# Norms over features: squares of four feature tiles kept together, their four products with ones issued beside each other

## The chip, the cores and the metric

The kernel runs as one program on 1 core of one Trainium2 chip. The metric is device microseconds of one execution; all traces are of one profiled execution. The engines are named as in the profile: PE is TensorE's matmul, PEld its weight load, DVE VectorE, ACT ScalarE, POOL GpSimd, SP SyncE, which issues most DMAs.

## The reference, cut to what matters

Two blocks of two layers each work on 256 context tokens and 256 latent tokens with 1024 features. Before and after every mixer and feed-forward network stands a root-mean-square norm over the features of a token:

```python
def _rms(x, gain, eps=1e-6):
    xf = x.astype(jnp.float32)
    y = xf * lax.rsqrt(jnp.mean(xf * xf, axis=-1, keepdims=True) + eps)
    return (y * gain.astype(jnp.float32)).astype(x.dtype)
```

Between the norms stand linear layers (a gated linear recurrence with attention, feed-forward networks, a second recurrence, latent attention with retention, a state-space mixer). All arithmetic is kept near fp32: each weight and each activation is split into a high and a low part, and a product is three matmuls.

## The kernel before, in words

Activations lie feature-major: a tile `x` is 128 partitions by 8 feature tiles (`KT`) by tokens. `SEGS` names the two halves of the tokens, context (256) and latent (256). The mean square over the features is therefore a sum over partitions and over 8 feature tiles. Class `Squares` makes it. `add` (L63) is called once for each feature tile: ACT squares 128x256 elements into a tile `sq` (L70), and `flush` (L72) multiplies the square of the feature tile before it with 32 columns of ones on PE (L77). Feature tile `k` writes the 32 PSUM partitions from `32 * (k % 4)` on, so that the eight products fill four strips, each twice. `flush` is called at the start of the next `add`, and once more by `all_rows` (L86), which copies the sums to SBUF (DVE, L94), turns them into one number per token on PE (L97), takes the reciprocal root in 11 short DVE instructions (`rstd_rows`, L407 to L420), and `rstd` (L105) broadcasts it over the partitions on PE (L111). The tiles `sq` share two buffers of pool `sm`.

A norm stands in one of two surroundings. In the first, `add` is called from the consumer of a linear layer: `linear_steps` (L213) loads a tile of weights (L257, 512 KB), ACT rounds it to `hi` (L195), DVE makes `lo` (L196), PE runs 24 matmuls (L205 to L207) or twice as many halves, and the consumer copies or adds the PSUM tile into `y` or `x` and squares it. Seven linear layers do that: both output projections of the first block, both last feed-forward parts of the first block, the output projection and the feed-forward network of layer one of the second block, and the gated layer of the last mixer. Where both halves of the tokens are done, the last three tiles run all context halves first and then all latent halves, and the context's norm starts between them. In the second surrounding, `residual_scaled` (L501 to L509), outside a linear layer's consumer, DVE scales a tile of `y`, POOL or DVE adds it to `x` (L508), and `add` squares the result. `halves` (L511) runs this for the context and then for the latent half, twice in the first block.

The order of the instructions on each engine is fixed when the program is built, by a list scheduler with a model of durations: where an engine would idle, it takes later work whose inputs and buffers are there. So the loads and matmuls of the second block's modulation vectors (`mods_steps`, L319: loads `mraw` of 512 KB at L326, four strips of matmuls at L329), which stand in the program text only in the mixer of the second layer, are put far ahead of it. That stream has 16 loads of `ada_w`, and its tiles share the two buffers named `mraw` of pool `mp`. During the feed-forward network of the second block's first layer, `mods_rows` (L370) holds both of these buffers, and later loads of modulation weights use pools of their own.

Of the kernel before, what the change touches and what calls it, by code (L numbers as in the profile page):

```python
# [9 lines left out]
F32 = mybir.dt.float32  # L10
F32R = mybir.dt.float32r
I32 = mybir.dt.int32
AF = mybir.ActivationFunctionType
# [4 lines left out]
P = 128  # L18
D = 1024
KT = 8  # L20
# [36 lines left out]
class Squares:  # L57


    def __init__(self, K, N, kt, rows, tag):  # L60
        self.K, self.N, self.kt, self.rows, self.tag, self.k, self.ps, self.sq = K, N, kt, rows, tag, 0, None, None

    def add(self, src):  # L63
        K, N, rows, k = self.K, self.N, self.rows, self.k
        if k == 0:
            self.ps = K.psum(self.tag)
        self.flush()
        self.k += 1
        self.sq = K.sm.tile([P, 512], F32, tag="sq", name=K.n("sq"), bufs=2)
        K.nc.scalar.activation(self.sq[:rows, :N], src, AF.Square)  # L70

    def flush(self):  # L72

        K, N, rows, k = self.K, self.N, self.rows, self.k - 1
        if self.sq is not None:
            j = k % 4
            K.nc.tensor.matmul(self.ps[32 * j:32 * j + 32, :N], K.ones[:rows, :32], self.sq[:rows, :N], start=k < 4,  # L77
                               stop=k + 4 >= self.kt, skip_group_check=True)
        self.sq = None

    def token_rows(self):

# [46 lines left out]
class Kern:  # L129
# [1555 lines left out]
    def ffn(self, X, N, Wu, Wd, kind, y, pool, hbufs=12, after=None, between=None,  # L1685
# [6 lines left out]
        for b, wd in enumerate(Wd):  # L1692
# [36 lines left out]

            last = b == len(Wd) - 1  # L1730
            self.linear_fm(wd, (hi, lo), N, add, tick=ticks[1], ends=last, half=half if last else None)


# [120 lines left out]
def second(K, tc, xd, s2, part, sc, m0, X, out):  # L1854
# [5 lines left out]
    with tc.tile_pool(name="s5w", bufs=1) as wpool:  # L1860
        with tc.tile_pool(name="ffn2", bufs=1) as fp:
# [11 lines left out]
            acc = K.squares(SEGS)  # L1873
            bc = []
            K.linear_fm(A["bw_out"], M, T, add, ends=True, half=lambda: bc.append(acc[0].rstd()))
            K.dbg("x2a", x)
            X = K.norm_tiles(T)
# [256 lines left out]
```

## Time and profile before

| what | value |
|---|---|
| median of 3 runs | 2568.2 us (2568.14 to 2576.02) |
| profiled execution | 2566.27 us |
| span of its trace | 2563.7 us |
| PE busy | 2414.7 us (94%), 15813 matmul instructions |
| DVE busy | 1518.1 us (59%) |
| ACT busy | 971.3 us (38%) |
| POOL busy | 503.0 us (20%) |
| moved by DMA | 378.04 MB, mean 147 GB/s |

The time of an execution is the span plus what lies around it (2.6 us in the profiled one). Every fp32 product appears as two weight loads and two matmul instructions, so that the 160 products of L77 with 256 tokens are 320 instructions. An engine's busy share is an average over stages with different limits; a matmul's end is modelled, and the start of the next one tells what it cost.

### The profile page before, as it was taken

How to read it: one execution, taken by the hardware profiler on the slowest of the kernel's cores; microseconds unless marked ns; L12 is line 12 of the kernel's file. 1: busy time of each engine (PE TensorE's matmuls, PEld its weight loads, DVE VectorE, ACT ScalarE, POOL GpSimd, SP SyncE). 2: the span in 40 equal slices, each digit the busy share in tenths (PEclk: the TensorE clock that was granted, in tenths of full speed). 3: DMA queues.
4: the chain of work that ended last, by engine and by line, in shares of the span. 5: the costliest groups of instructions: out<-in, count | busy, mean ns of one | idle time of the engine just before them, and what ended most of it. 6: DMA issues, size and time to landing. Idle time of an engine off the chain costs nothing.

```text
span 2563.7 us, 40161 instructions
## 1 busy us (share of the span) xinstructions
PE 2414.7 (94%) x15813; PEld 1970.4 (77%) x15813; DVE 1518.1 (59%) x2897; ACT 971.3 (38%) x1591; POOL 503.0 (20%) x648
## 2 busy tenths in 40 slices
PE   6999989999999998889999999999999999948999
PEld 5885566888888688887799696546888888627999
DVE  5545436777853656673655533654688734585666
ACT  5523323322222433333444444443423224534543
POOL 2810012556630233230100100110100000360000
PEclk8999999999999999999999999989999999989999
DMA  8326673555552332123855431003365533976554
GB/s 279 122 95 230 226 279 108 160 163 167 161 145 91 106 124 67 59 82 136 282 178 182 154 110 60 9 17 105 111 188 181 165 99 104 200 254 212 156 181 149
DMA packets 162924, 378.04 MB, mean 147 GB/s; under 512 B 24144, under 2 KB 70096, under 8 KB 162608
## 3 DMA queue, kind: packets, MB, share of 16 engines
q1 hardware_dynamic: 159728, 368.27, 45.0%
q0 software_dynamic: 3008, 7.21, 1.0%
q8 instruction: 124, 2.03, 0.3%
q14 instruction: 64, 0.52, 0.1%
HBM read 344.75 MB, written 30.67 MB: 146 GB/s over the span
## 4 chain that ended last, share of the span: by engine, by line
PE 79%; DVE 10%; DMA 4%; ACT 3%; issue 2%; POOL 1%; SPq 0%; DVEq 0%; ACTq 0%; POOLq 0%
PE pl L205 18%; PE pl L206 18%; PE pl L207 17%; PE pm L329 3%; PE pl L984 2%; PE pa L77 2%; DVE lo L196 2%; DMA mcol<-ada_t 2%; PE pl L279 1%; PE pl L280 1%; DVE pm L395 1%; PE pl L277 1%; PE pb L77 1%; PE pa L661 1%; PE pl L1006 1%
## 5 line engine op out<-in xcount | busy, mean ns | idle before, releaser
L195 ACT CAST hi<-raw 128x1024 fp32r<-128x1024 f32 (+4 forms) x393 | 400.4, 1020 | 847.1 <-PE pl L206 555.0
L196 DVE TENSOR_TENSOR lo<-raw,hi 128x1024 fp32r<-128x1024 f32 (+4 forms) x393 | 496.6, 1265 | 332.2 <-ACT hi L195 330.2
L206 PE MATMUL pl<-X,hi 128*128 128x256 f32 (+1 forms) x2032 | 649.2, 321 | 6.2 <-POOL X L490 5.7
L205 PE MATMUL pl<-X,hi 128*128 128x256 f32 (+1 forms) x2032 | 651.3, 322 | 1.8 <-ACT X L487 1.8
L207 PE MATMUL pl<-X,lo 128*128 128x256 f32 (+1 forms) x2032 | 647.6, 320 | 0.8 <-DVE lo L196 0.7
L206 PEld LDWEIGHTS pl<-X,hi 128*128 128x128 f32 x2032 | 392.6, 194 | 37.4 <-POOL X L490 8.7
L205 PEld LDWEIGHTS pl<-X,hi 128*128 128x128 f32 x2032 | 391.9, 194 | 36.3 <-issue 6.9
L207 PEld LDWEIGHTS pl<-X,lo 128*128 128x128 f32 x2032 | 392.5, 193 | 31.5 <-issue 4.9
L206 PE MATMUL pl<-hl,hi 128*128 128x256 f32 (+1 forms) x1071 | 326.8, 306 | 6.7 <-DVE hl L1713 6.6
L205 PE MATMUL pl<-hh,hi 128*128 128x256 f32 (+1 forms) x1071 | 329.5, 309 | 3.4 <-ACT hh L1712 3.2
L207 PE MATMUL pl<-hh,lo 128*128 128x256 f32 (+1 forms) x1071 | 325.9, 305 | 0.0
L205 PEld LDWEIGHTS pl<-hh,hi 128*128 128x128 f32 x1071 | 202.4, 189 | 25.6 <-issue 7.1
L206 PEld LDWEIGHTS pl<-hl,hi 128*128 128x128 f32 x1071 | 202.6, 189 | 18.9 <-DVE hl L1713 8.7
L207 PEld LDWEIGHTS pl<-hh,lo 128*128 128x128 f32 x1071 | 202.7, 189 | 10.5 <-issue 0.4
L205 PE MATMUL pl<-M,hi 128*128 128x256 f32 (+1 forms) x416 | 125.4, 303 | 7.4 <-ACT hi L195 6.4
L1505 POOL TENSOR_TENSOR Ec<-PGr,bc 128x576 f32<-128x576 f32 x64 | 95.5, 1503 | 169.8 <-DMA bc<-s_w 89.0
L329 PE MATMUL pm<-mraw,s_cc 128*32 128x512 f32 x576 | 115.7, 606 | 11.3 <-DMA mraw<-ada_w 10.9
L207 PE MATMUL pl<-M,lo 128*128 128x256 f32 (+1 forms) x416 | 122.2, 295 | 1.2 <-DVE lo L196 1.2
L206 PE MATMUL pl<-M,hi 128*128 128x256 f32 (+1 forms) x416 | 122.8, 296 | 0.2 <-DVE M L856 0.2
L1726 DVE TENSOR_TENSOR y<-y,pl 128x256 f32<-128x256 f32 (+1 forms) x86 | 45.1, 525 | 115.9 <-PE pl L207 115.5
L490 POOL TENSOR_TENSOR X<-nt,X 128x256 fp32r<-128x256 f32 x48 | 37.5, 781 | 382.7 <-ACT nt L489 382.7
L395 DVE SCALAR_TENSOR_TENSOR pm<-mcol,mrow 128x512 f32<-128x512 f32 x128 | 89.2, 697 | 34.0 <-DMA mcol<-ada_t 21.7
(515 smaller groups left out, 3753.5 us busy)
## 6 DMA issues: line engine op xcount, KB each, us to landing
mraw<-mod_w SPq DMA_DIRECT2D x96, 512.0 KB, 5.5
raw<-f_u SPq DMA_DIRECT2D x88, 512.0 KB, 4.3
mraw<-ada_w SPq DMA_DIRECT2D x64, 512.0 KB, 6.3
raw<-p_u SPq DMA_DIRECT2D x64, 512.0 KB, 3.7
raw<-p_d SPq DMA_DIRECT2D x64, 512.0 KB, 3.6
raw<-ow_fm SPq DMA_DIRECT2D x32, 512.0 KB, 3.3
mcol<-ada_t SPq DMA_DIRECT2D x64, 256.0 KB, 3.0
raw<-f_d SPq DMA_DIRECT2D x32, 448.0 KB, 3.3
```

Source lines behind the costliest of these rows:

```text
L77: K.nc.tensor.matmul(self.ps[32 * j:32 * j + 32, :N], K.ones[:rows, :32], self.sq[:rows, :N], start=k < 4, stop=k + 4 >= self.kt, skip_gro ...
L195: nc.scalar.copy(hi, raw)
L196: nc.vector.tensor_tensor(lo, raw, f32(hi), ALU.subtract)
L205: mm(out, w[0][:, kw, wsl], xh, start=first and a == 0, stop=False, skip_group_check=True)
L206: mm(out, w[0][:, kw, wsl], xl, start=False, stop=False, skip_group_check=True)
L207: mm(out, w[1][:, kw, wsl], xh, start=False, stop=last and a == nk - 1, skip_group_check=True)
L329: nc.tensor.matmul(ps[32 * j:32 * j + 32, :], s[:, k, :], raw[:, jj * 512:(jj + 1) * 512], start=k == 0, stop=k == KT - 1, skip_group_chec ...
L395: nc.vector.scalar_tensor_tensor(self.psum("pm"), buf[:, n % 2], 1.0, s[:, v], ALU.mult, ALU.mult, accum_out=(dst if h else part)[:, v, j: ...
L490: nc.gpsimd.tensor_tensor(lo[:, k, a:b], t, f32(hi[:, k, a:b]), ALU.subtract)
L984: nc.tensor.matmul(ps[:, :nk], q[:, tt * P:(tt + 1) * P], k[:, :nk], start=True, stop=True)
L1505: nc.gpsimd.tensor_tensor(Ec[i], ff[i], cs[i], ALU.mult)
L1726: nc.vector.tensor_tensor(y[:, c, a0:b0], y[:, c, a0:b0], ps, ALU.add)
```

## The change

`Squares` gets a group size: 4 where there are at most 256 tokens and 8 feature tiles, otherwise 1 as before. In a group the four squares go into the four quarters of one tile of 128x4x256, allocated as an `mraw` tile of pool `mp` (two buffers). `add` flushes only when four squares are waiting, and `flush` then issues the four products, which write four different strips of PSUM, one after the other. The number of squares and of products stays. The tile `sq` of pool `sm` is used by the three squares with 512 tokens and by other code, as before.

```diff
     def __init__(self, K, N, kt, rows, tag):
-        self.K, self.N, self.kt, self.rows, self.tag, self.k, self.ps, self.sq = K, N, kt, rows, tag, 0, None, None
+        self.K, self.N, self.kt, self.rows, self.tag, self.k, self.ps, self.sq = K, N, kt, rows, tag, 0, None, []
+        self.group = 4 if N <= 256 and kt == KT else 1
 
     def add(self, src):
         K, N, rows, k = self.K, self.N, self.rows, self.k
         if k == 0:
             self.ps = K.psum(self.tag)
-        self.flush()
+        if len(self.sq) == self.group:
+            self.flush()
         self.k += 1
-        self.sq = K.sm.tile([P, 512], F32, tag="sq", name=K.n("sq"), bufs=2)
-        K.nc.scalar.activation(self.sq[:rows, :N], src, AF.Square)
+        if self.group == 1:
+            sq = K.sm.tile([P, 512], F32, tag="sq", name=K.n("sq"), bufs=2)
+        elif not self.sq:
+            self.room = K.mp.tile([P, 4, 256], F32, tag="mraw", name=K.n("sq"), bufs=2)
+        if self.group > 1:
+            sq = self.room[:, len(self.sq)]
+        K.nc.scalar.activation(sq[:rows, :N], src, AF.Square)
+        self.sq.append((k, sq))
 
     def flush(self):
 
-        K, N, rows, k = self.K, self.N, self.rows, self.k - 1
-        if self.sq is not None:
+        K, N, rows = self.K, self.N, self.rows
+        for k, sq in self.sq:
             j = k % 4
-            K.nc.tensor.matmul(self.ps[32 * j:32 * j + 32, :N], K.ones[:rows, :32], self.sq[:rows, :N], start=k < 4,
+            K.nc.tensor.matmul(self.ps[32 * j:32 * j + 32, :N], K.ones[:rows, :32], sq[:rows, :N], start=k < 4,
                                stop=k + 4 >= self.kt, skip_group_check=True)
-        self.sq = None
+        self.sq = []
```

## Rows read from the trace of the kernel before

**Rows 1.** The page's chain that ended last: share of the span by engine, by line.
```profile
PE 79%; DVE 10%; DMA 4%; ACT 3%; issue 2%; POOL 1%; SPq 0%; DVEq 0%; ACTq 0%; POOLq 0%
PE pl L205 18%; PE pl L206 18%; PE pl L207 17%; PE pm L329 3%; PE pl L984 2%; PE pa L77 2%; DVE lo L196 2%; DMA mcol<-ada_t 2%; PE pl L279 1%; PE pl L280 1%; DVE pm L395 1%; PE pl L277 1%; PE pb L77 1%; PE pa L661 1%; PE pl L1006 1%
```
**Rows 2.** Groups of instructions, shapes apart: busy us, mean ns | idle before, releasers.
```profile
L77 PE MATMUL pa<-sq,ones 128*32 128x256 f32 x192 | 57.5, 398 | 12.5 <-ACT sq L70 12.1
...
L70 ACT ACTIVATE sq<-x 128x256 f32<-128x256 f32 x112 | 44.9, 414 | 103.1 <-POOL x L508 34.4 <-PE pa L77 20.8 <-PE pb L77 18.5
...
L77 PE MATMUL pb<-sq,ones 128*32 128x256 f32 x128 | 39.9, 418 | 6.8 <-ACT sq L70 6.7
```
**Rows 3.** Timeline of PE around 386 and 390 us: start, us, instruction.
```profile
385.73 0.39 PE L206 MATMUL pl<-M,hi 128*128 128x512 f32 x1
385.95 0.39 PE L207 MATMUL pl<-M,lo 128*128 128x512 f32 x1
386.27 0.62 PE L77 MATMUL pa<-sq,ones 128*32 128x256 f32 x2
...
387.25 0.39 PE L205 MATMUL pl<-M,hi 128*128 128x256 f32 x1
...
389.99 0.28 PE L206 MATMUL pl<-M,hi 128*128 128x256 f32 x1
390.11 0.28 PE L207 MATMUL pl<-M,lo 128*128 128x256 f32 x1
390.32 0.62 PE L77 MATMUL pa<-sq,ones 128*32 128x256 f32 x2
390.87 0.38 PE L205 MATMUL pl<-M,hi 128*128 128x256 f32 x1
```
**Rows 4.** Timeline from 339.66 us: 44 modulation matmuls in four strips.
```profile
339.66 4.90 PE L329 MATMUL pm<-mraw,s_cc 128*32 128x512 f32 x44
```
**Rows 5.** L77 alone in linear stretches: length, PE busy (instructions), PEld, clock, DMA, GB/s.
```profile
361.00:403.00 42.00, 7.30 (x26) 2.12 (x26) 1.00 0.45 151
...
1195.00:1212.00 17.00, 6.87 (x24) 1.89 (x24) 1.00 0.76 301
1414.00:1433.00 19.00, 3.71 (x12) 0.82 (x12) 1.00 0.43 139
...
1777.00:1818.00 41.00, 8.10 (x28) 2.17 (x28) 1.00 0.50 175
...
2160.00:2202.00 42.00, 7.92 (x28) 2.25 (x28) 1.00 0.61 126
...
2325.00:2360.00 35.00, 3.71 (x12) 0.82 (x12) 1.00 0.54 173
```
**Rows 6.** All engines in the first such stretch: PE, PEld, DVE, ACT, POOL busy.
```profile
361.00:403.00 42.00, 42.00 (x266) 34.00 (x265) 18.48 (x28) 9.67 (x19) 11.39 (x7) 1.00 0.45 151
```
**Rows 7.** Timeline of ACT and POOL at the end of two residual stretches.
```profile
426.20 0.84 POOL L508 TENSOR_TENSOR x<-x,nt 128x256 f32<-128x256 f32 x1 [0.49 <-DVE nt L507]
...
429.77 0.42 ACT L70 ACTIVATE sq<-x 128x256 f32<-128x256 f32 x1
853.62 0.84 POOL L508 TENSOR_TENSOR x<-x,nt 128x256 f32<-128x256 f32 x1 [0.30 <-DVE nt L507]
857.15 0.91 ACT L70 ACTIVATE sq<-x 128x256 f32<-128x256 f32 x2 [0.22 <-PE pa L77]
```
**Rows 8.** The stream into the `mraw` buffers: last load, L329 over a stretch, its next matmul.
```profile
433.07 0.62 SPq L326 DMA_DIRECT2D mraw<-ada_w  x1
...
442.00:813.00 371.00, 0.00 (x0) 0.00 (x0) 0.99 0.51 148
...
855.57 1.07 PE L329 MATMUL pm<-mraw,s_cc 128*32 128x512 f32 x8
```
**Rows 9.** The chain of waits near 1217 us: start, us, what.
```profile
1216.95 6.58 DMA mraw<-ada_w
```
**Rows 10.** L77 alone in a residual stretch, columns as in rows 5.
```profile
847.00:877.00 30.00, 11.25 (x38) 2.69 (x38) 0.89 0.42 138
```

## The prediction

> **What bounds the kernel now.** I read the chain that ended last first: the reader sees that PE carries 79% of it and that L77, the product of a square with ones, has 2% under `pa` and 1% under `pb` [rows 1]. The chain counts only time that set the end, so up to about 3% of 2563.7 us (77 us) hangs on L77. Next the groups of instructions: 192 + 128 = 320 instructions of L77, two for each product, kept PE busy for 57.5 + 39.9 = 97.4 us, and ACT's squares L70 sat idle for 20.8 + 18.5 us until an L77 had freed their buffer [rows 2]. The third view is PE's timeline in a linear layer: there PE goes from matmul to matmul and L77 lies between them [rows 3]. The fourth, all engines in that stretch, says whether anything else could be late if L77 were gone: PE is busy for all 42.00 us of it, DVE for 18.48, ACT for 9.67, and the DMA engines for 0.45 of the time [rows 6]. So these stretches are bound by PE, and a microsecond of PE there is one of the kernel.
>
> **What one interruption costs.** Starts tell it. Between two 256-token matmuls of the layer lie 390.11 - 389.99 = 0.12 us; with one product of L77 between them, 390.87 - 390.11 = 0.76 us. One product alone costs 0.64 us. Between 512-token matmuls the step is 385.95 - 385.73 = 0.22 us, and with a pair (one product for each half of the tokens) it is 387.25 - 385.95 = 1.30 us. A pair costs 1.07 us [rows 3]. The second product of a pair adds 1.07 - 0.64 = 0.43 us, so 0.43 us is the product and 0.21 us is paid once for each change from 128-column to 32-column matmuls and back.
>
> **What four products beside each other cost.** The trace before has that form in L329: four strips of 32 columns, fp32, each with moving data of its own. 44 of its instructions took 4.90 us, 0.111 us each, at 512 columns [rows 4]. At 256 columns I take half, so the eight instructions of a group take 8 x 0.056 = 0.45 us, as one product alone does now. The bounds: 0.43 us at the lower end (no group can be over before one of its products is) and 4 x 0.43 = 1.72 us at the upper end, if products of L77 should not overlap. I take 0.45, since L329 is the nearest row. A group therefore costs 0.64 us in a stream and a pair of groups 1.07 us, what one product and one pair cost before.
>
> The Trainium skill ("TensorE: Matmul & The Clock Gate", Part 3, measured speedup) puts the gain from four row strips at 3.07 times, below four. By that figure a group would take 1.72 / 3.07 = 0.56 us by my estimate, and all 40 groups together 4 us more than in my sum. The rate of 0.111 us in this trace is nearer to a full four, and I keep to it.
>
> **The linear stretches.** L77 has 26 instructions in the stretch from 361 to 403 us, as many from 813 to 847 us, then 24, 12, 28, 28 and 12 [rows 5]; with two instructions a product and the order pair or single that PE's timeline shows, these are 18 pairs and 42 singles: 18 x 1.07 + 42 x 0.64 = 46.1 us. With groups, five stretches (both halves, or two accumulators) keep a pair of groups at the fifth feature tile, the two others keep one group there, and in the four layers that split their last tiles the context's last group still falls inside the stream: 5 x 1.07 + 6 x 0.64 = 9.2 us. The stretches give back 46.1 - 9.2 = 36.9 us. The last group adds nothing at its end: today one product follows the last square, then four side by side do, in the same time. What is late next is the split of the weights, with DVE at 44% and ACT at 23% of the stretch [rows 6], so I leave the 36.9 whole.
>
> **The residual stretches.** There DVE, POOL, ACT and PE pass tiles on. POOL's last addition ends at 426.20 + 0.84 = 427.04 us, but the last square ends at 429.77 + 0.42 = 430.19 us; in the first block's second norm of that kind, 854.46 and 858.06 [rows 7]. Each square now needs a buffer of two, and one of the two often holds a square of the other half that waits for its layer's end, so that ACT waits for PE at nearly every tile. With a tile of four, ACT waits once for each group. The last square can follow the last addition by some 0.5 us, which is 2.6 and 3.1 us earlier; against it stands one group that has to be over before the next four start (0.64 us). I take 2.5 us for each of the four half norms of the first block's first layer and 1 us for each of the two norms of its second layer: 12 us. Bounds: 0, if the squares only wait elsewhere, and the 39.3 us of ACT's waits for `x` squares [rows 2]. The kernel's first norm waits for its inputs, and I count nothing there.
>
> **The buffers.** The new tile takes an `mraw` buffer. Where nothing else lives in those two, this is free. In the first layer it isn't: the last load of the hoisted modulation stream before the long feed-forward network is issued at 433.07 us, no L329 runs from 442 to 813 us, and the next one starts at 855.57 us [rows 8]. Two loads thus sat in both buffers for some 420 us, since PE had no hole to spend on them, and the squares of the stretch from 813 us on will ask for just these buffers. Nothing in the trace before shows a square that waits for such a load. Below, it costs nothing (or gains, if hoisted matmuls no longer get between the norm's); above, it costs what the second rival says. I take 5 us.
>
> Sum: 36.9 + 12 - 5 = 44 us off the profiled execution of 2566.3 us, 2522 us. The median of the runs shown is 1.9 us higher, so I predict 2524 us.
>
> **Rivals.**
> A. Starved squares. If the two `mraw` buffers are full when a layer's first square comes, no square runs until PE has spent the parked loads, at the end of the stream. Then 16 squares at 0.41 us and two pairs of groups stand ahead of the norm, 6.6 + 2.1 us, in place of one square and one product, 1.0 us: 7.7 us lost at each of the two first-layer layers, 15 in all, and some 7 us of the residual gain with it. 2524 + 22 = 2546 us. For it: the parked loads [rows 8]. Against it: the stream itself loses its interruptions even so, and at the first of the two layers both buffers may be free.
> B. The products don't overlap. Then only the 0.21 us of a change is saved, at 60 - 11 = 49 places, 10 us, and a third of the 12 us in the residual stretches: 2554 us. Against it stands L329 [rows 4].
> C. The clock. With L77 gone from the residual stretches, PE idles more there. From 847 to 877 us the granted clock was 0.89 of the full 2.4 GHz in the mean, so it stood at the lower level of 1.2 GHz for 0.22 x 30 = 6.6 us of it [rows 10]. If that doubled in eight such stretches, half of 6.6 us lost in each would be 26 us: 2550 us. Against it: in a residual stretch PE mostly waits for others, and a slow clock costs only what is on the path. The Trainium skill ("TensorE: Matmul & The Clock Gate", Part 1) says that an idle PE falls to 1.2 GHz, which is the rule behind this rival; the granted clock below 1 in rows 10 agrees.
> D. Slower than before. The hoisted stream loses its buffers to the squares, so that its loads no longer run early; 14 of its 16 then come two at a time where PE must wait for them in order. One such wait is in the trace: 6.58 us for a load [rows 9], and with 0.9 us for its matmuls seven rounds make 52 us, 2576 us. It turns the sign from the sixth round on (6 x 7.5 = 45 against 44). Against it: the stream is needed late, and its matmuls can lie between linear layers that cover the loads.
> E. No change. If the stretches were bound by weights rather than by PE, the interruptions would only turn into waits, and the residual gain less the buffers, 7 us, would be left: 2561 us. Against it: PE has no idle time from 361 to 403 us [rows 6].
>
> **How the numbers follow.** Forecast 0.64, with a range of its own from 2508 (the residual gain twice as large, no cost of buffers) to 2540; A 0.17, B 0.05, C 0.05, D 0.05, E 0.04. From 2506 to 2552 us lie nearly all of the forecast's 0.64 but for some 0.04 at its ends, most of A, and half of C: about 0.78. A measurement of this kernel can't tell 0.3%, some 8 us, from no change. Faster by more than that: the forecast, A, B and C, less a tail of 0.02, 0.89. Within it: E and a tail, 0.06. Slower: D, 0.05.
>
> **What would show it.** Right: the count of 320 stays, but L77 is busy for 25 to 35 us; in PE's timeline eight L77 instructions start within some 0.5 us; the stretch of rows 3 has one pair of groups in place of four pairs, and the step from the layer's last matmul before it to the first after it is still near 1.3 us; the seven stretches are 3 to 7 us shorter each. ACT's squares hardly wait for L77. Wrong: steps of 2 us and more around a group (B); squares from 813 us on that all start after the layer's last matmul and just after an L329 (A); waits of several us for `mraw<-ada_w` in the second layer (D); L205 to L207 with unchanged starts although L77 is gone (E).

## The result, and the profile after

The changed kernel takes 2533.6 us (median of four runs, 2532.6 to 2535.2) against 2568.2 (four runs, 2565.2 to 2576.0): ratio 0.9861, 95% interval 0.9839 to 0.9884. The forecast was 2524 with a range of 2506 to 2552. The profiled execution took 2535.2 us with a span of 2533.4, 30.3 us less than the span before; the forecast had taken 44 off. The line numbers are eight higher than before from the new code on: the product is L85, the square L77, the three matmuls L213 to L215, the stream's load and matmul L334 and L337.

The page's chain by line, the answer to the second line of [rows 1], no longer names the product with ones among its fifteen costliest; its shares by engine add up to 64% only, so that they are not to be set beside those of before:

```profile
PE 48%; DVE 9%; DMA 3%; ACT 2%; issue 2%; POOL 0%; DVEq 0%; ACTq 0%; POOLq 0%
PE pl L214 12%; PE pl L213 12%; PE pl L215 11%; DMA mcol<-ada_t 2%; DVE lo L204 2%; PE pm L337 1%; DVE pm L403 1%; PE pa L909 1%; PE pl L992 1%; PE pl L287 1%; PE pa L1023 1%; DMA mraw<-ada_w 1%; PE pl L285 1%; PE pl L288 1%; PE pb L1289 1%
```

Now the groups of instructions that answer to [rows 2] (busy us, mean ns, then idle time before them and what ended it):

```profile
L77 ACT ACTIVATE sq<-x 128x256 f32<-128x256 f32 x112 | 42.2, 410 | 75.4 <-POOL x L516 33.4 <-DVE x L1908 14.2 <-DVE x L1877 11.9
...
L85 PE MATMUL pa<-sq,ones 128*32 128x256 f32 x192 | 33.6, 406 | 12.6 <-DVE pp L1326 10.5 <-ACT sq L77 1.9
...
L85 PE MATMUL pb<-sq,ones 128*32 128x256 f32 x128 | 24.6, 459 | 8.1 <-ACT sq L77 8.1
```

The same 320 instructions keep PE busy for 33.6 + 24.6 = 58.2 us instead of 97.4, and PE no longer stands among the three costliest releasers of the squares: ACT waits for the tiles of `x` themselves. All waits of these squares for the product add up to 5.1 us, where they were 59.3 us before. PE's timeline, at three places, answers to [rows 3]:

```profile
379.63 0.39 PE L214 MATMUL pl<-M,hi 128*128 128x512 f32 x1
379.86 0.39 PE L215 MATMUL pl<-M,lo 128*128 128x512 f32 x1
380.18 0.64 PE L85 MATMUL pa<-sq,ones 128*32 128x256 f32 x8
380.63 0.61 PE L85 MATMUL pb<-sq,ones 128*32 128x256 f32 x8
381.18 0.39 PE L213 MATMUL pl<-M,hi 128*128 128x256 f32 x1
...
390.01 0.63 PE L85 MATMUL pa<-sq,ones 128*32 128x256 f32 x6
...
391.15 0.28 PE L214 MATMUL pl<-M,hi 128*128 128x256 f32 x1
391.36 0.62 PE L85 MATMUL pa<-sq,ones 128*32 128x256 f32 x2
391.91 0.39 PE L215 MATMUL pl<-M,lo 128*128 128x256 f32 x1
...
2315.99 0.28 PE L215 MATMUL pl<-M,lo 128*128 128x256 f32 x1
2316.20 0.64 PE L85 MATMUL pa<-sq,ones 128*32 128x256 f32 x8
2316.77 0.38 PE L213 MATMUL pl<-M,hi 128*128 128x256 f32 x1
2317.00 0.28 PE L214 MATMUL pl<-M,hi 128*128 128x256 f32 x1
```

From the last matmul before a pair of groups to the first after it are 381.18 - 379.86 = 1.32 us, less the usual 0.22: sixteen instructions cost 1.10 us, where a pair of single products cost 1.07. At 2316.20 a whole group stands alone: 2316.77 - 2315.99 - 0.12 = 0.66 us, where one product cost 0.64. The place between shows a group that did not stay whole: three of its products ran at 390.01, the fourth 1.35 us later, for another 391.91 - 391.15 - 0.12 = 0.64 us.

One more thing stands in these rows that the forecast's price leaves out. The matmul behind an interruption is followed after 2317.00 - 2316.77 = 0.23 us and not after 0.12, and so it was before, where the line behind the last one of [rows 3] is

```profile
391.09 0.28 PE L206 MATMUL pl<-M,hi 128*128 128x256 f32 x1
```

with 391.09 - 390.87 = 0.22 us. Each interruption therefore cost some 0.10 us more than the 0.64 or 1.07 us that the forecast took, before and after alike.

L85 alone in four linear stretches answers to [rows 5], and all engines in the first of them to [rows 6] (PE, PEld, DVE, ACT, POOL):

```profile
361.00:400.00 39.00, 2.94 (x26) 0.84 (x26) 1.00 0.38 122
...
1775.00:1811.00 36.00, 3.57 (x32) 0.99 (x32) 0.95 0.36 121
2154.00:2190.00 36.00, 3.58 (x32) 0.99 (x32) 0.92 0.87 142
2310.00:2340.00 30.00, 1.89 (x16) 0.45 (x16) 0.97 0.57 176
```
```profile
361.00:400.00 39.00, 38.85 (x279) 34.22 (x278) 21.93 (x36) 11.10 (x21) 14.57 (x11) 1.00 0.38 122
```

PE is still busy nearly all of the time, with DVE at 56% and ACT at 28%: the stretch is shorter and bound by the same engine. The end of a residual stretch of the same norm as in the second half of [rows 7]. The lines there are of the context half; here are the context half (two lines) and the latent half (two lines) of the changed kernel:

```profile
838.64 0.84 POOL L516 TENSOR_TENSOR x<-x,nt 128x256 f32<-128x256 f32 x1 [0.30 <-DVE nt L515]
...
841.76 1.02 ACT L77 ACTIVATE sq<-x 128x256 f32<-128x256 f32 x3
...
854.89 0.84 POOL L516 TENSOR_TENSOR x<-x,nt 128x256 f32<-128x256 f32 x1 [0.49 <-DVE nt L515]
855.76 1.03 ACT L77 ACTIVATE sq<-x 128x256 f32<-128x256 f32 x3 [0.91 <-POOL x L516]
```

and the latent half of the kernel before:

```profile
871.77 0.83 POOL L508 TENSOR_TENSOR x<-x,nt 128x256 f32<-128x256 f32 x1 [0.49 <-DVE nt L507]
...
874.62 0.42 ACT L70 ACTIVATE sq<-x 128x256 f32<-128x256 f32 x1 [0.40 <-PE pb L77]
```

In the context half the last square ended 858.06 - 854.46 = 3.60 us after POOL's last addition before, and 842.78 - 839.48 = 3.30 us now; in the latent half it was 875.04 - 872.60 = 2.44 us and is 856.79 - 855.73 = 1.06 us. In the norm ahead of the network the lag is 4.05 us where it was 3.72 (context), and 3.35 where it was 3.15 (latent). So one of four halves got clearly shorter.

The other side of the balance is the modulation stream of [rows 8]. Four lines of SP's queue, then L337 alone in two stretches:

```profile
855.15 0.33 SPq L334 DMA_DIRECT2D mraw<-ada_w  x1
...
896.84 0.90 SPq L334 DMA_DIRECT2D mraw<-ada_w  x2
...
908.39 3.62 SPq L334 DMA_DIRECT2D mraw<-ada_w  x2
...
942.95 2.22 SPq L334 DMA_DIRECT2D mraw<-ada_w  x2
```
```profile
442.00:813.00 371.00, 0.00 (x0) 0.00 (x0) 0.99 0.52 150
...
900.00:960.00 60.00, 16.33 (x56) 2.11 (x56) 0.94 0.57 187
```

Before, eight of the 16 loads were issued from 369 to 433 us and six more from 857 to 875, and two came in the mixer. Now two are issued at 855 and 858 us and 14 from 896.84 to 945 us, inside the second layer's mixer. The chain of waits there, the answer to [rows 9]:

```profile
914.94 0.98 PE pm L337 x4
915.92 0.32 PE pl L287
916.83 1.01 PE pm L337 x4
917.86 6.39 DMA mraw<-ada_w
924.29 1.05 PE pm L337 x4
...
931.56 5.97 DMA mraw<-ada_w
```

Where the time went is read best by one mark that all kernels share: the n-th rounding of a weight tile on ACT (L195 before, L203 after). The table gives its start less its start before; negative is ahead. "Again" is a second execution of the changed kernel; the other columns are the experiments below.

| mark, us before | changed | again | linear only | residual only | late | two | mix | thin | once |
|---|---|---|---|---|---|---|---|---|---|
| 163.5 | -3.0 | -5.4 | -6.6 | -4.1 | -4.6 | -9.6 | -9.1 | -6.8 | -2.0 |
| 402.3, first output projection nearly done | -7.5 | -10.6 | -11.3 | -3.9 | -4.3 | -12.2 | -12.7 | -11.4 | -6.7 |
| 809.4, network's last tiles | -8.8 | -12.5 | -10.1 | -1.9 | -2.3 | -15.2 | -12.0 | -13.3 | -8.6 |
| 896.5, mixer begins | -17.4 | -21.2 | -17.7 | -5.7 | -5.6 | -21.5 | -17.0 | -22.0 | -17.9 |
| 954.5, stream over | +1.0 | -1.7 | -2.2 | +10.3 | +10.9 | -19.1 | -15.6 | -15.4 | -15.5 |
| 1194.6 | +1.0 | -2.5 | -3.2 | +9.5 | +12.7 | -19.0 | -14.7 | -14.1 | -15.2 |
| 1248.1, next residual stretch done | -6.7 | -11.2 | -10.7 | +10.4 | +14.7 | -21.0 | -21.7 | -22.2 | -23.5 |
| 2563.7, end | -30.3 | -33.6 | -34.3 | +6.0 | +13.7 | -33.3 | -45.3 | -44.7 | -37.4 |

From 896.5 to 954.5 the changed kernel gives back 18.4 us, its second execution 19.5. That loss was the main thing to explain. Each column is one execution, and the same code does not take the same time in each: from 1194.6 to the end "changed", "again" and "once" have the same code and win 31.3, 31.1 and 22.2 us. Differences of a few us between two columns are therefore no reading by themselves.

### The profile page after: what moved, and what is told of

It reads as the page before. It is cut to its first block, busy times and chain, and to the rows that moved or that the text cites. A ratio compares the mean times of both kernels' runs of the same rounds, so it can differ in the third digit from the quotient of the medians.

```text
span 2533.4 us, 40092 instructions
## 1 busy us (share of the span) xinstructions
PE 2379.4 (94%) x15813; PEld 1959.2 (77%) x15813; DVE 1522.6 (60%) x2897; ACT 967.0 (38%) x1591; POOL 509.0 (20%) x648
## 4 chain that ended last, share of the span: by engine, by line
PE 48%; DVE 9%; DMA 3%; ACT 2%; issue 2%; POOL 0%; DVEq 0%; ACTq 0%; POOLq 0%
PE pl L214 12%; PE pl L213 12%; PE pl L215 11%; DMA mcol<-ada_t 2%; DVE lo L204 2%; PE pm L337 1%; DVE pm L403 1%; PE pa L909 1%; PE pl L992 1%; PE pl L287 1%; PE pa L1023 1%; DMA mraw<-ada_w 1%; PE pl L285 1%; PE pl L288 1%; PE pb L1289 1%
## 5 line engine op out<-in xcount | busy, mean ns | idle before, releaser
L203 ACT CAST hi<-raw 128x1024 fp32r<-128x1024 f32 (+4 forms) x393 | 400.3, 1020 | 840.1 <-PE pl L214 510.0
L213 PE MATMUL pl<-X,hi 128*128 128x256 f32 (+1 forms) x2032 | 651.9, 323 | 2.1 <-ACT X L495 1.9
L215 PE MATMUL pl<-X,lo 128*128 128x256 f32 (+1 forms) x2032 | 647.0, 319 | 0.0
L213 PEld LDWEIGHTS pl<-X,hi 128*128 128x128 f32 x2032 | 391.4, 193 | 39.8 <-issue 9.0
L215 PEld LDWEIGHTS pl<-X,lo 128*128 128x128 f32 x2032 | 392.3, 193 | 32.4 <-issue 6.6
L213 PE MATMUL pl<-hh,hi 128*128 128x256 f32 (+1 forms) x1071 | 327.6, 307 | 4.7 <-ACT hh L1720 4.6
L215 PE MATMUL pl<-hh,lo 128*128 128x256 f32 (+1 forms) x1071 | 325.6, 305 | 0.0
L213 PEld LDWEIGHTS pl<-hh,hi 128*128 128x128 f32 x1071 | 202.4, 189 | 20.8 <-ACT hh L1720 5.8
L215 PEld LDWEIGHTS pl<-hh,lo 128*128 128x128 f32 x1071 | 202.9, 190 | 10.3 <-issue 0.8
L337 PE MATMUL pm<-mraw,s_cc 128*32 128x512 f32 x576 | 120.0, 618 | 13.2 <-DMA mraw<-ada_w 13.0
L213 PE MATMUL pl<-M,hi 128*128 128x256 f32 (+1 forms) x416 | 122.9, 298 | 6.1 <-ACT hi L203 5.2
L215 PE MATMUL pl<-M,lo 128*128 128x256 f32 (+1 forms) x416 | 122.3, 296 | 1.2 <-DVE lo L204 1.2
L403 DVE SCALAR_TENSOR_TENSOR pm<-mcol,mrow 128x512 f32<-128x512 f32 x128 | 89.3, 698 | 33.3 <-DMA mcol<-ada_t 22.5
```

Of the source, the lines that this page charges most:

```text
L203: nc.scalar.copy(hi, raw)
L213: mm(out, w[0][:, kw, wsl], xh, start=first and a == 0, stop=False, skip_group_check=True)
L215: mm(out, w[1][:, kw, wsl], xh, start=False, stop=last and a == nk - 1, skip_group_check=True)
L337: nc.tensor.matmul(ps[32 * j:32 * j + 32, :], s[:, k, :], raw[:, jj * 512:(jj + 1) * 512], start=k == 0, stop=k == KT - 1, skip_group_chec ...
L403: nc.vector.scalar_tensor_tensor(self.psum("pm"), buf[:, n % 2], 1.0, s[:, v], ALU.mult, ALU.mult, accum_out=(dst if h else part)[:, v, j: ...
```

## The experiments

**All products into one strip.** The groups stay, but every product writes the same 32 partitions, so that four can't lie beside each other.

```diff
-            j = k % 4
+            j = 0 if self.group == 4 else k % 4
...
```

> Groups of four as in the change, but all eight products of a norm go to the same strip of 32 PSUM partitions, so that they can't run beside each other. If running side by side is what makes a group cheap, a group costs 4 x 0.43 + 0.21 = 1.92 us in place of 0.65: 16 groups in the linear stretches add 20 us, and up to 12 groups that end a norm add up to 15 us more: 2554 to 2569 us. If the gain came from fewer changes between matmul shapes and fewer waits for buffers alone, the time stays at 2534 to 2540 us.

2547.8 us (six runs), ratio 0.9918 (0.9890 to 0.9945): between the two. PE's timeline around a pair of groups in this kernel:

```profile
1784.12 0.39 PE L216 MATMUL pl<-M,lo 128*128 128x512 f32 x1
1784.43 1.91 PE L85 MATMUL pa<-sq,ones 128*32 128x256 f32 x8
1786.19 1.89 PE L85 MATMUL pb<-sq,ones 128*32 128x256 f32 x8
1788.01 0.39 PE L214 MATMUL pl<-M,hi 128*128 128x256 f32 x1
```

The pair costs 1788.01 - 1784.12 - 0.22 = 3.67 us in place of 1.10. So strips are what makes a group as cheap as one product (in one strip the products also add up in one place of PSUM; the run does not tell the two apart). Four pairs one by one cost 4 x 1.07 = 4.28 us, so that this kernel should still gain by its smaller number of changes between 128 and 32 columns; that this is the rest of its gain is argued and not measured. Its total lies in neither of the two ranges.

**Linear consumers alone, residual stretches alone.** `squares` gets a size of 4 or 1 for each of the two surroundings.

```diff
-        new = self.squares(segs)
+        new = self.squares(segs, 1)
...
-        new = self.squares(SEGS)
+        new = self.squares(SEGS, 1)
```

> Groups of four only where a linear layer's consumer makes the squares; groups of one in the residual stretches. If the two terms of the prediction add up, the residual term of about 12 us is lost: 2540 to 2548 us. If the residual stretches gave nothing by themselves, 2530 to 2537 us.

2537.0 us (four runs), ratio 0.9879 (0.9845 to 0.9912): at the upper edge of the second reading. The interval is some 17 us wide, so the medians alone don't exclude a few us for the residual stretches. The trace says more: in the six stretches that hold squares (they are listed further down) this kernel is 39.3 us shorter than before, the changed one 44.9 and 45.7.

> The opposite: groups of four only in the residual stretches, groups of one in the linear layers. By the prediction's terms 2568 - 12 = 2556 us, less what the modulation stream loses; 2552 to 2566 us. If the residual stretches were the larger part of the gain, below 2550 us.

2571.5 us (ten runs), ratio 1.0020 (1.0003 to 1.0037): not faster at all, outside what was expected. The table shows why: from 809.4 to 896.5 it wins 3.8 us, as much as the kernel "late" below, which groups nothing but has no stream there; from 1194.6 to 1248.1 it wins nothing (9.5 to 10.4), where the linear part alone wins 7.5. And its groups, too, push the stream into the mixer, where it loses 16.0 us. Counted in the traces, PE goes 72 times from a layer's matmuls to the squares' products and back before, 70 times here, 30 times in "linear only" and 26 in the changed kernel: in the residual stretches the products are issued as their squares come, and the groups hardly hold together (at 398.82, 400.28, 401.38 and 402.37 us of the changed kernel four products of one group ran alone).

**No groups in the first layer's linear consumers.** Groups of one in the output projection and the network ahead of the mixer, and in the norms behind them; groups of four elsewhere.

```diff
-        self.group = 4 if N <= 256 and kt == KT else 1
+        self.group = 4 if N <= 256 and kt == KT and K.grouped else 1
...
```

> As the change, but groups of one, in the old small tiles, in the output projection and the feed-forward network of the first layer, where the hoisted modulation stream wants the two large buffers. If the squares there push that stream into the second layer's mixer, the stretch up to 955 us gets back its 18 us and the first layer's linear and residual stretches lose about as much (some 17 us): 2530 to 2538 us, with modulation matmuls again at 414 to 434 and 855 to 875 us. If the 18 us in the mixer have another cause, they stay, and the time is near 2551 us.

2530.9 us (four runs), ratio 0.9853 (0.9812 to 0.9893), as expected if the squares displace the stream. The loads are back at 368 to 432 and 856 to 874 us, and the stretch from 896.5 to 954.5 loses 3.4 us instead of 18.4. At its end this kernel is 1.3 us behind the one before, the changed kernel 1.0: all that the groups win ahead of the mixer is lost in it. (The profiled execution, 2544.1 us, is the longest of the four.)

**Late loads without groups.** The kernel before, and each `ada_w` load of that stream waits for one element of the second layer's normalised input.

```diff
+                if gate is not None:
+                    nc.vector.tensor_copy(raw[:, :1], gate)
                 nc.sync.dma_start(raw, W[l, k * P:(k + 1) * P, g * 2048 + h * 1024:g * 2048 + (h + 1) * 1024])
```

> The kernel before, with one thing added: each of the 16 ada_w loads of the second layer's modulation stream waits for a copy of one element of that layer's normalised input, so that none of them can run in the first layer's output projection or in the FFN's end, where 14 of the 16 run before. Nothing is grouped. If the 18.4 us that the changed kernel gives back between the times 897 and 955 come from those loads being displaced into the second layer's mixer, this kernel loses most of them in the same stretch (12 to 20 us), may win 3 to 5 us in the first layer's norms, out of which the stream's matmuls go, and ends at 2576 to 2586 us. If the give-back has another cause (the groups of four themselves, a buffer that the mixer wants), that stretch stays within 5 us of before and the time near 2567.

2585.8 us (four runs), ratio 1.0082 (1.0054 to 1.0111), as expected if the displaced loads are the cause; the stretch in question loses 16.5 us (-5.6 to +10.9). Nothing was grouped here, so the late loads alone make the loss.

**The stream ahead of the network, with and without groups.** It starts ahead of the first layer's feed-forward network, one step after each feature tile.

```diff
+            n0, grp = K.mods(s2, A["ada_w"], K.ada_b, 0, "n0")
+            K.bg["m"] = K.mods_stream([(s2, A["ada_w"], 0, 0, n0, K.ada_b)])
...
-                  ... half=half, ticks=("w", "w"))
+                  ... half=half, ticks=("wm", "wm"))
```

> The changed kernel, with the first stream of modulation products (ada_w, 16 loads and 64 products) started ahead of the first layer's FFN, a step of it after each of that FFN's feature tiles, instead of in the second layer's mixer. There it lies beside a stretch that TensorE bounds, so its own products are to be paid: 64 at about 0.22 us is 14 us if each runs alone, 4 to 7 us if they run four beside each other as the kernel has them. If the loads' late place is what the mixer paid for, the stretch from 897 to 955 wins 16 to 20 us against the changed kernel, the FFN pays 5 to 12, and the time is 2520 to 2530. If the give-back of 18 us has another cause, or the FFN's own weight loads wait behind the new ones on SyncE's queue, the time is 2534 or more.

2533.4 us (four runs), ratio 0.9886 (0.9859 to 0.9913), no better than the changed kernel: above the first reading's range, just short of the second's. The mixer did lose nothing (+5.1 to +3.8), but from 402.3 to 494.4 the network paid 21.6 us, far more than the 5 to 12 expected. L337 alone in that kernel:

```profile
405.00:500.00 95.00, 19.81 (x64) 2.72 (x64) 0.91 0.52 158
```

Its products ran at 19.81 / 64 = 0.31 us an instruction, not at the 0.111 of [rows 4].

> The kernel before with that same move of the modulation stream into the first layer's FFN, and nothing grouped. In the kernel before the stream runs for nothing in two places where TensorE waits anyway, but 16 of its products wait for the mixer; if the displacement theory holds, the move wins little here (the mixer loses nothing to it before) and pays the FFN's products: 2562 to 2572, and the changed kernel with the move is 36 to 48 us faster than this one, as the prediction's terms without a loss of buffers would have it (about 44). If the move is simply better in both, 2550 to 2558.

2570.5 us (ten runs), ratio 1.0024 (1.0005 to 1.0043), inside the first reading, and 37 us above the kernel with groups. With the stream out of the mixer in both, the groups are worth 37 us. The move does not cost both the same: from 402.3 to 494.4 this kernel is 14.6 us slower than the one before, and the kernel with groups 21.6 us; why, no run shows.

**Loads or products?** Why does a late stream cost 16 to 20 us? "Thin" keeps its loads and cuts 56 of 64 products to 16 columns; "once" keeps the products and leaves out 14 of 16 loads.

```diff
+                    n = 16 if thin and k else 512
...
+                if once is None or k == 0:
                     raw = pool.tile([P, 1024], F32, tag=tag, name=self.n("mraw"), bufs=bufs)
```

> The changed kernel, with all 16 loads of the second layer's first modulation stream as they are, but 56 of its 64 products cut from 512 columns to 16 (so that part of that layer's modulation is left out of the sum). If what the mixer pays for the displaced stream is TensorE's time for its products, the stretch from 897 to 955, which loses 18 to 20 us in the changed kernel, loses 4 to 9 us here, and the time is 2520 to 2526. If it pays for waits on the loads, it still loses 14 to 20 us there and the time is 2530 to 2537.

> The other half of the same question: the changed kernel with all 64 products at full width, but only 2 of the 16 loads; 14 steps of the stream use a tile that is already there (so that most of the modulation weights are left out). The two loads wait for one element of the second layer's normalised input, so that the products stay in the mixer. If the mixer pays for TensorE's time, it loses 14 to 20 us between 897 and 955 as before and the time is 2530 to 2537; if it pays for waits on loads, it loses 4 to 9 us and the time is 2518 to 2526. If each pays half, both kernels lose about 10.

Thin: 2524.7 us (four runs), ratio 0.9852 (0.9829 to 0.9876), 6.6 us lost from 896.5 to 954.5, as expected if products are what costs. Once: 2527.6 us, between its two ranges, ratio 0.9861 (0.9838 to 0.9883), 2.4 us lost, which by that same theory should have been 14 to 20. The totals don't tell these kernels from the changed one (0.9861, and 0.9889 in its second measurement); the stretch does, with 6.6 and 2.4 us against 18.4 and 19.5. Either half alone is cheap, so neither theory stands alone. The products of the stream, alone in the same 60 us, show what may join them: thin, then once, then two places in PE's timeline of once.

```profile
900.00:960.00 60.00, 3.44 (x56) 2.06 (x56) 0.93 0.60 193
```
```profile
900.00:960.00 60.00, 5.63 (x48) 1.11 (x43) 0.94 0.27 88
```
```profile
911.91 1.92 PE L340 MATMUL pm<-mraw,s_cc 128*32 128x512 f32 x16
919.71 1.92 PE L340 MATMUL pm<-mraw,s_cc 128*32 128x512 f32 x16
```

With the data there, 16 instructions run together in 1.92 us, 0.12 us each. In the changed kernel each load brings two products, which run alone as four instructions in 0.98 to 1.05 us, 0.25 each (the chain shown above): 16.33 us for 56 instructions against 5.63 for 48; at 0.12 us each the 56 would take 6.7 us, so some 10 us go with the pairs. Products at full width are dear, by this reading, because the loads come one by one and break them into pairs of strips, and each pair is an interruption of its own. It is the effect that the change is about, on the other side. The reading is worked out from these rows; no run kept all loads and issued the products in sixteens.

**Groups of two in the old room.** A tile of 2 x 256 columns under the name `sq`, so that no square takes an `mraw` buffer.

```diff
-            self.room = K.mp.tile([P, 4, 256], F32, tag="mraw", name=K.n("sq"), bufs=2)
+            self.room = K.sm.tile([P, 2, 256], F32, tag="sq", name=K.n("sq"), bufs=2)
```

> Groups of two instead of four, in the two-buffer room that the squares had before (a tile of 2 x 256 columns in the small pool), so that no square takes a buffer from the modulation stream. Four interruptions for each half norm instead of two (four of eight), each with two products beside each other. If an interruption costs a fixed 0.12 to 0.21 us of switching and its products hide behind each other, a group of two costs 0.22 + 0.1 = about 0.35 us more or less, so that the linear stretches keep about 26 of their 37 us, and with the stream's loads where they were before no 18 us are given back: 2538 to 2548. If the room in the stream's buffers isn't what gives time back, the stretch from 897 to 955 loses as in the changed kernel and the time is 2552 or more.

2534.0 us (four runs), ratio 0.9879 (0.9850 to 0.9908): a little better than expected, and equal to groups of four. The mixer loses 2.4 us (-21.5 to -19.1); the rest of the kernel wins less than with four (14.3 us from 1194.6 on, against 31.3, and against the 22.2 of "once").

**The mixture, and the changed kernel beside it.** Groups of two up to the end of the first layer's network, groups of four from there.

```diff
+        self.group = 2
...
+         K.group = 4
```

> Groups of two, in the squares' old room, up to the end of the first layer's FFN, where the modulation stream runs in the norms' idle stretches; groups of four in the stream's buffers from the second layer on, as in the changed kernel. If the loss of the stream's buffers is the whole give-back and the rest is a price per interruption, it takes the groups-of-two kernel's 19 us up to 1195 and the changed kernel's 31 us from there: about 50 us less than before, 2514 to 2520, below both. If the gains up to 1195 of the groups of two were chance between executions (they are 11 us above what halved interruptions give), 2522 to 2530.

> The changed kernel as it is, beside the mixture on the same chip: 2530 to 2537, and the stretch from 897 to 955 loses 16 to 20 us again. Should that loss not come back, it was chance of one execution and the reading of the give-back falls.

Mixture 2518.4 us (four runs, 2514.6 to 2523.0), ratio 0.9822 (0.9800 to 0.9845); the changed kernel on the same chip 2534.6 (six runs, 2529.4 to 2540.7), ratio 0.9889 (0.9867 to 0.9910). It beats both, as expected, and "again" shows the loss in the mixer again, 19.5 us. Against the kernel before on that chip, 2561.5 us, the changed kernel wins 26.9 us there and not the 34.6 of its first measurement. The stream's products in the mixture:

```profile
836.00:860.00 24.00, 7.06 (x24) 1.50 (x24) 0.79 0.51 173
...
900.00:960.00 60.00, 3.17 (x16) 0.45 (x16) 0.92 0.32 106
```

Only 16 instructions of the stream are left in the mixer, which loses 1.4 us (-17.0 to -15.6); from 1194.6 to the end it wins 30.6 us, as much as the changed kernel.

## Why the prediction was right, and where its sizes were not

*The price of a group.* Right: 0.64 us for one product and 1.07 for a pair were to be the price of one group and of a pair of groups; the trace shows 0.66 and 1.10. Both leave out the 0.10 us behind each interruption. The Trainium skill ("TensorE: Matmul & The Clock Gate", Part 3, measured speedup) has 3.07 times for four row strips. The strips here are of output columns (128*32 in the rows); with the 0.21 us of a change taken off, one strip against four strips is here (3.67 - 0.21) / (1.10 - 0.21) = 3.9 times for a pair of groups, and the measurement decides. Rival B (no overlap) is refuted by the timeline, and the one-strip kernel shows what it would have looked like.

*The linear stretches, 36.9 us, and the residual stretches, 12 us.* The stretches that hold both (163.5 to 494.4, 809.4 to 896.5, 1194.6 to 1248.1, 1403.6 to 1472.3, 1774.4 to 1839.5 and 2161.0 to 2362.3 us) got 44.9 us shorter, 45.7 in the second execution; 3.3 of it, from 809.4 to 896.5, also comes in the kernel "late", because the stream has left. That leaves about 42 of the 49 us.

The linear term was right in size, as far as one execution tells. "Linear only" has the same six stretches 39.3 us shorter, and at most 3.3 of that is the stream's, so that 36 to 39 us stand against 36.9. By the steps in the timelines two errors in it nearly cancel, which was luck: 0.10 us more at each of 60 - 11 = 49 places would have added 4.9 us, and PE was interrupted at 16 places and not at 11, since the context's last group did not stay whole (it ran in pieces of six and two instructions), which at 0.74 us takes 3.7 us away.

The residual term was too large. The residual stretches add 5.6 or 6.4 us to "linear only", some of which can be the stream's absence, and "residual only" shows nothing beyond that absence: between nothing and some 6 of the 12 us came. The step that failed is that the last square would follow the last addition by 0.5 us. ACT's waits for the products did go, from 59.3 to 5.1 us, but the lag stayed at 3.3 to 4.1 us in three of four half norms and fell to 1.06 us in one. In the context halves the fifth square waits 2.45 and 1.98 us for its buffer, and then ACT rounds a tile of weights (L203) ahead of the last squares; in the latent half of the norm ahead of the network it copies a tile of other work (L1465) first. That the products were issued as their squares came, some alone, also fits that L85 was busy for 58.2 us and not for the 25 to 35 us forecast. The forecast's two lags in [rows 7] are of a latent and of a context half, which are not alike.

*The buffers, 5 us.* This term was mis-sized by some 10 us. The price was 18.4 us in the mixer, less the 3.3 us that the first layer wins when the stream is gone: 15.1 us. The forecast had seen that two loads parked in the `mraw` buffers would collide with the squares, and thought of the squares as those who wait. It was the reverse: the squares of the output projection got the buffers first, and the stream's loads did not run at all until 855 us. That is rival D's mechanism (14 of 16 loads in the mixer), with a price of 18 us in place of its 52: two waits of 6 us stand in the chain and not seven. Waits alone don't make the 18 us either, since "thin", which keeps all loads and has waits of 6.24 and 7.13 us for them in its chain, loses 6.6; the other 12 us come only with the products at full width. Rival A's starved square appeared once, in the second layer:

```profile
1216.56 0.42 ACT L77 ACTIVATE sq<-x 128x256 f32<-128x256 f32 x1 [5.10 <-PE pm L337]
```

It waits 5.10 us for a matmul of a modulation stream (5.27 in "again"). The stretch from 1194.6 to 1248.1 that holds it still got 7.7 us shorter.

*The first norm, nothing.* The changed kernel is 3.0 and 5.4 us ahead at 163.5, but two kernels without groups there ("late", "residual only") are 4.6 and 4.1 ahead, and a third ("early" without groups) is 0.6 behind. Executions without groups thus differ by 5 us at this mark, and no gain of the first norm can be told from that. Both kernels with groups of two lead by over 9 us there, 2 us more than any other; that stays unexplained.

*The sum.* 41.6 - 15.1 + 3.0 = 29.5 of the 30.3 us of span. The forecast was 49 - 5 = 44.

*The clock, rival C.* It did fall. The residual stretch that had 0.89 in [rows 10] now shows (L85 alone, columns as there):

```profile
842.00:872.00 30.00, 6.42 (x26) 1.79 (x26) 0.72 0.32 106
```

At 0.72, 0.56 x 30 = 16.8 us are at 1.2 GHz instead of 6.6. The stretch from 809.4 to 896.5 got shorter by 8.6 us all the same; what the lower clock cost in it no run measured by itself. The mean over the span is 0.963 against 0.966.

*No change, rival E.* Refuted: the stretches shortened and stayed bound by PE.

## What to carry to other kernels

Count the interruptions of a stream of wide matmuls, not the narrow products in them: products that write different strips cost as much as one if they are issued together, and a loader that delivers their data piece by piece can take that back. Before a new tile borrows a buffer that is shared with work that the scheduler pulls ahead, ask where that work runs for nothing today and what it costs where it must go; here a smaller group in its own room was better in those places, and the larger one elsewhere. When a wait of one engine is taken away, look at what the engine does next before you count the gain: here 54 us of ACT's waits went, and other work of ACT's kept the last square as late in three halves of four. And compare a half with the same half.

## What the runs showed of the hardware

An interruption of PE by 32-column products has one price for one, two or four products side by side: 0.64 and 0.66 us in the timeline of the changed kernel, with 0.10 us more behind it. Two of them, in the kernel with groups of two:

```profile
381.57 0.28 PE L215 MATMUL pl<-M,lo 128*128 128x256 f32 x1
381.77 0.63 PE L85 MATMUL pa<-sq,ones 128*32 128x256 f32 x4
382.33 0.39 PE L213 MATMUL pl<-M,hi 128*128 128x256 f32 x1
```

That is 382.33 - 381.57 - 0.12 = 0.64 us. And it pays to have the data of all four strips there together: 512-column products ran at 0.12 us an instruction in sixteens over four strips (1.92 us) and at 0.25 in fours over two strips (0.98 us).
